# Gate and up with a fourth mixed pair per unit, and the first weight sum of a pair made by accumulating transfers

## The chip, the cores and the metric

The kernel runs on one core of one Trainium2 chip. The metric is the device time in microseconds (us) of one execution. Engines are named as in the profile: PE is the matmul engine (TensorE), DVE is VectorE, ACT is ScalarE, POOL is GpSimd, SP is SyncE, which here only issues loads.

## What is computed

A decoder trunk of two layers on 256 tokens of width 2048, float32. Layer 0 is a Mamba-2 mixer, layer 1 sliding-window attention, and each layer ends in the same feed-forward block, which is what the change touches:

```python
D_MODEL, SEQ, DEPTH, D_FF = 2048, 256, 2, 5632

def swiglu(u, w_gate, w_up, w_down):
    return (jax.nn.silu(u @ w_gate) * (u @ w_up)) @ w_down

for layer in range(DEPTH):
    ...                                                    # mixer or attention, norms, residual
    ffn = swiglu(rmsnorm(h, g[2]), ffn_w_gate[layer], ffn_w_up[layer], ffn_w_down[layer])
    h = h + rmsnorm(ffn, g[3])
```

## The kernel before

**Products.** Float32 accuracy is made of three matmuls: each weight tile and each activation tile is split into a high and a low part (hi = cast, lo = tile - hi), and a block product is hi x hi, hi x lo, lo x hi, each a 128x128 by 128x512 matmul. The high part of a weight is a cast on ACT into `whi` (L136), the low part a subtraction on DVE into `wlo` (L137). There are four buffers of each (`CVB`), and `Weights.next` converts up to three parts ahead of the one that PE uses. Raw weights come from memory through SP's queue into five buffers `raw` (`RAWB`), loaded up to four tiles ahead.

**Units.** Gate and up are done in 11 units of 512 columns per layer. The first unit is plain. In units 1 to 10 the 16 slices of the contraction (2048 = 16 x 128) form eight pairs 0 to 7 of an even and an odd slice. A plain pair is two items, "A" (gate) and "B" (up): each 2 slices x 2 halves of the tokens x 3 = 12 matmuls, from one raw tile of 512 KB and one conversion of 128x1024. A mixed pair, item "M", does the same 2x2x2 block product with seven products in the place of eight (Strassen's scheme): 21 matmuls. Its weights come in four parts that are converted one after the other:

- "a": gate's even slice and up's odd slice (raw tile `ta`), 6 matmuls
- "g": gate's odd slice (half of raw tile `tb`, whose other half is up's even slice), 3 matmuls
- "13": the tile `t13` = `ta` + up's even slice, added to both halves, 6 matmuls
- "24": the tile `t24`, first half `t13`'s first half + up's odd slice, second half that + gate's odd slice, 6 matmuls

The sums are three additions on DVE (L114, in `_sums`), issued right after the conversion of "g". `t13` and `t24` have one buffer each, in the pool `mixed` of the layer. The activations' mixed forms of each pair (`sx`) are computed once per layer by `mixed_x` and reused by all units; those calls are spread over the items of the first unit's "up" by a hook, every other item.

**Order.** The list `UNIT` sets the order on PE and thereby that of loads and conversions: A and B of pair 3, M0, A and B of 4, M1, A and B of 5, M2, then "E" (L447 to L451, where ACT and DVE combine finished products), then A and B of 6 and 7. After E, `store_half` transposes half of the last unit's result after each "B". A unit ends with four additions (L871), two SiLU (L873) and two products (L875).

**Queues.** SP issues all weight loads in order. POOL has only small work in these stages, and its queue's transfers are the spill and fetch of the residual `h` (L688, L695) outside of the units. Engines and queues run their instructions in order; a new use of a buffer waits until the last reader of the old contents has ended. The down projection and the mixer's output projection use mixed pairs too, with the same class `Weights`, and aren't touched.

Of the kernel before, what the change touches and what calls it, by code (L numbers as in the profile page):

```python
# [8 lines left out]
F32 = mybir.dt.float32  # L9
F32R = mybir.dt.float32r  # L10
AF = mybir.ActivationFunctionType
ALU = mybir.AluOpType
AX = mybir.AxisListType

P = 128
# [6 lines left out]
FF = 5632  # L22
KF = FF // P
EPS = 1e-6
NH = 64
CW = 512
# [1 line left out]
SUB = 2  # L28
RAWB = 5
CVB = 4  # L30
SPAIRS = 3


def both(*pairs):
    return [(c, i) for i in pairs for c in "AB"]
# [15 lines left out]

UNIT = both(3) + [("M", 0)] + both(4) + [("M", 1)] + both(5) + [("M", 2), ("E", 0)] + both(6, 7)
DOWN = [pair_order(KF, 6, 8, 3, 4), pair_order(KF, 8, 2, 2, 4)]
WOUT = [pair_order(DI // P, 3, 13, 3, 2), pair_order(DI // P, 6, 2, 2, 3)]

# [1 line left out]
class Weights:  # L59
# [6 lines left out]
    def __init__(self, nc, pool, specs, scaled, raw_ahead=RAWB - 1, cv_ahead=CVB - 1):  # L66
        self.nc, self.pool, self.specs, self.scaled = nc, pool, specs, scaled
        self.raw_ahead, self.cv_ahead = raw_ahead, cv_ahead
        self.subs, self.first = [], {}
        for i, (key, ap) in enumerate(specs):  # L70
            if isinstance(ap, tuple):
                if ap[0] == "b":
                    for part in ("a", "g", "13", "24"):
                        self.subs.append((i, part, SUB, CW, key + part))
                continue
            a = ap.shape[1]
            n = ap.shape[2]
            per = (SUB * CW) // n
            for s in range(0, a, per):
                self.first.setdefault(key, len(self.subs))  # L80
                self.subs.append((i, s, per, n, key))
        self.raw = []
        self.cv = []
        self.pin = lambda ins: ins
        self.pos = 0

    def _load(self, upto):
        while len(self.raw) < min(upto, len(self.specs)):
            key, ap = self.specs[len(self.raw)]
            if isinstance(ap, tuple):  # L90
                t = self.pool.tile([P, 2, CW], F32, tag="raw", name="raw", bufs=RAWB)
                for k in range(2):
                    self.nc.sync.dma_start(t[:, k : k + 1, :], ap[1 + k])
            else:
                _, a, n = ap.shape
                t = self.pool.tile([P, a, n], F32, tag="raw", name="raw", bufs=RAWB)
                self.nc.sync.dma_start(t[:], ap)
            self.raw.append(t)

    def _mixed(self, i, part):  # L100
# [2 lines left out]
        return {"a": lambda: ta[:], "g": lambda: tb[:, 0:1, :], "13": lambda: self.t13[:],  # L103
                "24": lambda: self.t24[:]}[part]()

    def _sums(self, i):

        ta, tb = self.raw[i - 1], self.raw[i]
        t13, t24 = [self.spool.tile([P, 2, CW], F32, tag="t%d" % n, name="t%d" % n) for n in (13, 24)]
        self.t13, self.t24 = t13, t24  # L110
        for o, p, q in ((t13[:], ta[:], tb[:, 1:2, :].broadcast_to([P, 2, CW])),
                        (t24[:, 0, :], t13[:, 0, :], ta[:, 1, :]),
                        (t24[:, 1, :], t24[:, 0, :], tb[:, 0, :])):
            self.keep(self.nc.vector.tensor_tensor(o, p, q, ALU.add))  # L114

    def _convert(self, upto):
# [42 lines left out]
def tile_yoco(ctx: ExitStack, tc: tile.TileContext, a: dict):  # L159
# [48 lines left out]
    def add_ffn(l):  # L208
        wg, wu = a["ffn_w_gate"][l], a["ffn_w_up"][l]
        for u in range(FF // CW):  # L210
            if u == 0:
                add("gate%d_%d" % (l, u), wg, KD, CW * u)
                add("up%d_%d" % (l, u), wu, KD, CW * u)
                continue
            add_pairs("unit%d_%d" % (l, u), UNIT, (wg, CW * u), (wu, CW * u))
        wd = a["ffn_w_down"][l]
# [16 lines left out]

    W = Weights(nc, wpool, specs, scaled)
    W.keep = tc.keep_in_program_order

    def bank():
        return psum.tile([P, CW], F32, tag="bank", name="bank")
# [142 lines left out]
    def mixed_x(x, i, o, tmp):  # L381


        y = tmp[:, 0, :].rearrange("p (k t) -> p k t", k=2)
        f = tmp[:, 1, :].rearrange("p (n t) -> p n t", n=4)
        ks = slice(SUB * i, SUB * i + 2)
        nc.vector.tensor_tensor(y, x[0][:, ks, :].bitcast(F32), x[1][:, ks, :].bitcast(F32), ALU.add)
        e0, e1, o0, o1 = y[:, 0, :P], y[:, 0, P:], y[:, 1, :P], y[:, 1, P:]
        for n, p, q in ((1, e1, o1), (3, e0, e1), (2, e0, f[:, 1, :]), (0, o0, f[:, 2, :])):
            nc.vector.tensor_tensor(f[:, n, :], p, q, ALU.subtract)  # L390
        split_bank(o[:, :, 0, :], o[:, :, 1, :], f)
# [165 lines left out]
    xt = new_xt()  # L557
# [253 lines left out]
    def row_factor():  # L811

        return [norm_stats(hpool, h[1], t) for t in range(NT)]
# [17 lines left out]
    def ffn(layer, mix):  # L831
        xt = new_xt()
        xh, xl, _ = xt
        with tc.tile_pool(name="ffn%d" % layer, bufs=1, side="right") as fp:
            hid = [fp.tile([P, KF, T], F32R, tag=n, name=n) for n in ("hh", "hl")]
            spool = tc.tile_pool(name="mixed%d" % layer, bufs=1, side="right")
            scr = hpool.tile([P, 2 * NT, CW], F32, tag="gpost", name="scr")
            todo = []

            def hook():  # L840
                if todo:
                    f = todo.pop(0)
                    if f is not None:
                        f()

            def store_half(u, t):

                pt = bank()
                for k in range(4):
                    nc.tensor.transpose(pt[:, P * k : P * (k + 1)], scr[:, NT + t, P * k : P * (k + 1)], ident[:])  # L850
                ts = slice(P * t, P * (t + 1))
                ks = slice(4 * u, 4 * u + 4)
                split_bank(hid[0][:, ks, ts], hid[1][:, ks, ts], pt[:].rearrange("p (k t) -> p k t", k=4))

            def store(u):
                for t in range(NT):
                    store_half(u, t)

            def unit(u):

                pp = Pairs("unit%d_%d" % (layer, u), UNIT, xt, lambda i: sx[:, i])
                terms = [scr[:, 0, :], scr[:, 1, :], vh[:, 0, :], vh[:, 1, :]]
                stores = []
                for n, item in enumerate(UNIT):
                    pp.item(item, terms)
                    if item[0] == "E":
                        stores = [0, 1]
                    elif stores and item[0] == "B":
                        store_half(u - 1, stores.pop(0))
                for name, part in zip(Pairs.OUT, terms):  # L870
                    nc.vector.tensor_tensor(part, pp.bk[name][:], part, ALU.add)  # L871
                for t in range(NT):
                    nc.scalar.activation(scr[:, t, :], scr[:, t, :], AF.Silu, scale=rs[t][:, 0:1])  # L873
                for t in range(NT):
                    nc.vector.scalar_tensor_tensor(scr[:, NT + t, :], vh[:, t, :], rs[t][:, 0:1], scr[:, t, :],  # L875
                                                   ALU.mult, ALU.mult)

            rs = None
            for u in range(FF // CW):
                if u:  # L880
                    unit(u)
                    continue
                gb = a_first("gate%d_%d" % (layer, u), mix, gt[:, layer, 2, :], xt)
                rs = row_factor()
                spill_h()
                sp = spool.__enter__()
                W.spool = sp
                sx = sp.tile([P, SPAIRS, 4, 2, P], F32R, tag="sx", name="sx")
                vh = sp.tile([P, 2, CW], F32, tag="vh", name="vh")
                for i in range(SPAIRS):  # L890
                    todo += [None, lambda i=i: mixed_x(xt, i, sx[:, i], sp.tile([P, 2, CW], F32, tag="t13", name="yf"))]
                for t in range(NT):
                    nc.scalar.activation(scr[:, t, :], gb[t][:], AF.Silu, scale=rs[t][:, 0:1])
                ub = a_form("up%d_%d" % (layer, u), xt, KD, hook=hook)
                for t in range(NT):
                    nc.vector.scalar_tensor_tensor(scr[:, NT + t, :], ub[t][:], rs[t][:, 0:1], scr[:, t, :],
                                                   ALU.mult, ALU.mult)
            spool.__exit__(None, None, None)
            spool = tc.tile_pool(name="down%d" % layer, bufs=1, side="right")
            W.spool = dp = spool.__enter__()  # L900
            todo += [None, lambda: store(FF // CW - 1)]

            def close():
                spool.__exit__(None, None, None)
                fetch_h()

            mix = Stage("down%d" % layer, DOWN, hid).run(Mix(layer, 3), dp, close, todo, 2 if layer == 0 else CVB)
            return mix
# [14 lines left out]
    with tc.tile_pool(name="attn", bufs=1, side="right") as ap:  # L923
        xt = new_xt()
# [506 lines left out]
```

## Time and profile before

| | |
|---|---|
| median of 3 runs | 2361.01 us (2360.69 to 2361.43) |
| the profiled execution's own time | 2360.69 us |
| its span, first to last instruction | 2358.8 us |
| PE busy | 2338.6 us, 99% |
| DVE busy | 2031.0 us, 86% |
| ACT busy | 1403.3 us, 59% |
| POOL busy | 91.3 us, 4% |
| DMA | 462.24 MB, mean 196 GB/s |

A row of a group of instructions reads: line, engine, operation, output <- inputs, shape, count, then busy us and mean ns of one, then the engine's idle time before them and what ended it. A row of the timeline reads: start in us, duration, engine, line, operation; in brackets the idle time before it and what ended that. A row of waits reads: who waited <- for whom: us in total, times, longest. A row of windows reads: stretch, its length, then busy us (and count) of PE, PEld (weight load into PE), DVE, ACT, POOL, then the granted clock of PE, the busy share of the DMA engines and GB/s. A row of one line's instructions gives minimum, median and maximum ns, then first and last start; "DMA to landing" is the time from issue until the data has landed.

### The profile page before, as it was taken

To read this page: it belongs to the slowest core of one execution; us is meant where nothing else is said; L and a number is where in the kernel's file an instruction comes from. 1 tells how busy PE (TensorE), PEld (TensorE's weight loads), DVE (VectorE), ACT (ScalarE), POOL (GpSimd) and SP (SyncE) were. 2 spreads that over 40 slices of the span, in tenths; PEclk is the share of its full clock that TensorE was granted. 3 is DMA by queue.
4 is the path that set the end of the run, shared out by engine and by line. 5 is a ranking of instruction groups with operands and counts; after the bars stand their busy time and mean duration, and the time that the engine had idled before them with its cause. 6 is when DMAs were issued, how large, how long until landed. Compare 5 with 4: busy or idle time off the path is not lost.

```text
span 2358.8 us, 32303 instructions
## 1 busy us (share of the span) xinstructions
PE 2338.6 (99%) x11519; PEld 1941.8 (82%) x11519; DVE 2031.0 (86%) x2878; ACT 1403.3 (59%) x1983; POOL 91.3 (4%) x76
## 2 busy tenths in 40 slices
PE   9999999999999999999999999999999999999998
PEld 8888888888878888888888878777888888888886
DVE  6998887878987999999998878965899999999786
ACT  6576766665565555555555567754555555555554
POOL 2500000000000000000000000000000000000000
PEclk9999999999999999999999999999999999999999
DMA  7576666657666666566666765436665665666675
GB/s 227 161 225 196 189 188 194 189 171 243 195 205 196 196 196 206 188 204 207 214 190 199 206 236 169 135 127 186 198 199 193 206 211 185 200 205 202 199 209 192
DMA packets 288673, 462.24 MB, mean 196 GB/s; under 512 B 20208, under 2 KB 118768, under 8 KB 286720
## 3 DMA queue, kind: packets, MB, share of 16 engines
q1 hardware_dynamic: 286752, 449.30, 61.3%
q0 software_dynamic: 1472, 10.55, 1.2%
q8 instruction: 90, 1.47, 0.3%
q14 instruction: 71, 0.58, 0.1%
q10 hardware_dynamic: 288, 0.33, 0.0%
HBM read 453.76 MB, written 6.36 MB: 195 GB/s over the span
## 4 chain that ended last, share of the span: by engine, by line
PE 94%; DVE 3%; ACT 1%; issue 1%; DMA 0%; POOL 0%; DVEq 0%; SPq 0%; ACTq 0%; POOLq 0%
PE bank L420 20%; PE bank L418 20%; PE bank L419 20%; PE bank L318 13%; PE bank L323 7%; PE bank L376 3%; PE bank L377 3%; PE bank L378 3%; DVE wlo L137 1%; PE bank L850 1%; PE bank L1119 1%; PE bank L1294 1%; DVE acc L1050 1%; PE bank L613 1%; PE bank L1330 0%
## 5 line engine op out<-in xcount | busy, mean ns | idle before, releaser
L137 DVE TENSOR_TENSOR wlo<-raw,whi 128x1024 fp32r<-128x1024 f32 (+1 forms) x785 | 883.6, 1155 | 162.9 <-ACT whi L136 154.7
L136 ACT CAST whi<-raw 128x1024 fp32r<-128x1024 f32 (+1 forms) x785 | 771.0, 999 | 422.1 <-PE bank L420 243.7
L318 PE MATMUL bank<-xx,whi 128*128 128x512 f32 (+1 forms) x1488 | 521.3, 396 | 0.0
L136 ACT CAST whi<-t 128x1024 fp32r<-128x1024 f32 x194 | 204.5, 1054 | 358.4 <-DVE t L114 230.0
L323 PE MATMUL bank<-xx,wlo 128*128 128x256 f32 (+1 forms) x1488 | 414.6, 284 | 0.9 <-DVE wlo L137 0.9
L418 PE MATMUL bank<-whi,xx 128*128 128x512 f32 x980 | 384.9, 393 | 0.0
L420 PE MATMUL bank<-whi,xx 128*128 128x512 f32 x980 | 382.1, 390 | 0.0
L419 PE MATMUL bank<-wlo,xx 128*128 128x512 f32 x980 | 381.6, 389 | 0.0
L318 PEld LDWEIGHTS bank<-xx,whi 128*128 128x128 f32 (+1 forms) x1488 | 275.7, 187 | 61.6 <-issue 0.3
L137 DVE TENSOR_TENSOR wlo<-t,whi 128x1024 fp32r<-128x1024 f32 x194 | 237.0, 1222 | 72.0 <-ACT whi L136 70.9
L323 PEld LDWEIGHTS bank<-xx,wlo 128*128 128x128 f32 (+1 forms) x1488 | 279.4, 188 | 11.5 <-issue 5.2
L418 PE MATMUL bank<-whi,hh 128*128 128x512 f32 x564 | 219.8, 390 | 0.0
L420 PE MATMUL bank<-whi,hl 128*128 128x512 f32 x564 | 219.4, 389 | 0.0
L419 PE MATMUL bank<-wlo,hh 128*128 128x512 f32 x564 | 219.4, 389 | 0.0
L420 PEld LDWEIGHTS bank<-whi,xx 128*128 128x128 f32 x980 | 184.0, 188 | 38.8
L419 PEld LDWEIGHTS bank<-wlo,xx 128*128 128x128 f32 x980 | 184.1, 188 | 37.4
L418 PEld LDWEIGHTS bank<-whi,xx 128*128 128x128 f32 x980 | 184.0, 188 | 37.0
L114 DVE TENSOR_TENSOR t<-t,raw 128x512 f32<-128x512 f32 x194 | 134.1, 691 | 5.8
L420 PEld LDWEIGHTS bank<-whi,hl 128*128 128x128 f32 x564 | 105.9, 188 | 22.2
L419 PEld LDWEIGHTS bank<-wlo,hh 128*128 128x128 f32 x564 | 105.9, 188 | 21.9
L418 PEld LDWEIGHTS bank<-whi,hh 128*128 128x128 f32 x564 | 105.9, 188 | 21.6
L114 DVE TENSOR_TENSOR t<-raw 128x1024 f32<-128x1024 f32 x97 | 118.2, 1218 | 0.0
(240 smaller groups left out, 3212.0 us busy)
## 6 DMA issues: line engine op xcount, KB each, us to landing
raw<-in_ssm_w_in_dram SPq DMA_DIRECT2D x161, 512.0 KB, 4.6
raw<-in_ffn_w_down_dram SPq DMA_DIRECT2D x120, 512.0 KB, 5.5
raw<-in_ffn_w_gate_dram SPq DMA_DIRECT2D x116, 512.0 KB, 4.7
raw<-in_ffn_w_up_dram SPq DMA_DIRECT2D x116, 512.0 KB, 3.9
raw<-in_ffn_w_gate_dram SPq DMA_DIRECT2D x120, 256.0 KB, 3.8
raw<-in_ffn_w_up_dram SPq DMA_DIRECT2D x120, 256.0 KB, 4.1
raw<-in_ffn_w_down_dram SPq DMA_DIRECT2D x112, 256.0 KB, 4.6
raw<-in_ssm_w_out_dram SPq DMA_DIRECT2D x46, 512.0 KB, 4.9
```

Of the source, the lines that this page charges most:

```text
L114: self.keep(self.nc.vector.tensor_tensor(o, p, q, ALU.add))
L136: self.pin(nc.scalar.copy(hi[:], src))
L137: self.pin(nc.vector.tensor_tensor(lo[:], src, hi[:].bitcast(F32), ALU.subtract))
L318: nc.tensor.matmul(o, wh, xx[:, kt, :, :].rearrange("p a t -> p (a t)"), start=(kt == 0), stop=(kt == kts - 1))
L323: nc.tensor.matmul(o[:, :T], wl, xx[:, kt, 0, :], start=False, stop=False)
L376: nc.tensor.matmul(o, sh, wh, start=(kt == 0), stop=False)
L377: nc.tensor.matmul(o, sh, wl, start=False, stop=False)
L378: nc.tensor.matmul(o, sl, wh, start=False, stop=(kt == kts - 1))
L418: nc.tensor.matmul(o, s[0], wh, start=(n == 1), stop=False)
L419: nc.tensor.matmul(o, s[0], wl, start=False, stop=False)
L420: nc.tensor.matmul(o, s[1], wh, start=False, stop=(n == self.total[name]))
L613: nc.tensor.matmul(o[:], hi[:, kk, cs], xr[2][:, kt, :, :].rearrange("p a t -> p (a t)"), start=(kt == 0), stop=(kt == KD - 1))
```

## The change

Pair 3 becomes a fourth mixed pair (the list before has pairs 0 to 2 mixed and 3 to 7 plain). The order of a unit becomes A4 B4 M0 A5 B5 M1 A6 M2 B6 M3 E A7 B7: pairs 0 to 3 are mixed, 4 to 7 plain. After E the halves of the last result are stored after A7 and after B7. `t13` is no longer added on DVE in units 1 to 10: when a pair's second raw tile is loaded, `_first_sums` has GpSimd's queue load gate's even and up's odd slice into `t13` (two transfers of 256 KB) and then add up's even slice to both halves with one accumulating transfer (512 KB). The two sums that give `t24` stay on DVE. The fourth pair's `sx` lies in the last four slices of the first hidden tile, which are written only by the last unit; `mixed_x` takes its scratch from `t24`'s buffer instead of `t13`'s and is called four times per layer instead of three. Down and output projections keep the addition on DVE.

```diff
-SPAIRS = 3
+SPAIRS = 4
...
-UNIT = both(3) + [("M", 0)] + both(4) + [("M", 1)] + both(5) + [("M", 2), ("E", 0)] + both(6, 7)
+UNIT = both(4) + [("M", 0)] + both(5) + [("M", 1), ("A", 6), ("M", 2), ("B", 6), ("M", 3), ("E", 0)] + both(7)
...
+        self.by_dma = set()
+        self.t13s = []
...
                     self.nc.sync.dma_start(t[:, k : k + 1, :], ap[1 + k])
+                if ap[0] == "b" and key in self.by_dma:
+                    self._first_sums(len(self.raw))
...
+    def _first_sums(self, i):
+
+        (_, ge, uo), (_, _, ue) = self.specs[i - 1][1], self.specs[i][1]
+        t13 = self.spool.tile([P, 2, CW], F32, tag="t13", name="t13")
+        for k, ap in enumerate((ge, uo)):
+            self.nc.gpsimd.dma_start(t13[:, k : k + 1, :], ap)
+        self.nc.gpsimd.dma_start(t13[:], ue.broadcast_to([P, 2, CW]), accum_op=ALU.add)
+        self.t13s.append(t13)
+
     def _sums(self, i):
 
         ta, tb = self.raw[i - 1], self.raw[i]
-        t13, t24 = [self.spool.tile([P, 2, CW], F32, tag="t%d" % n, name="t%d" % n) for n in (13, 24)]
+        if self.specs[i][0] in self.by_dma:
+            t13 = self.t13s.pop(0)
+        else:
+            t13 = self.spool.tile([P, 2, CW], F32, tag="t13", name="t13")
+            self.keep(self.nc.vector.tensor_tensor(t13[:], ta[:], tb[:, 1:2, :].broadcast_to([P, 2, CW]), ALU.add))
+        t24 = self.spool.tile([P, 2, CW], F32, tag="t24", name="t24")
         self.t13, self.t24 = t13, t24
-        for o, p, q in ((t13[:], ta[:], tb[:, 1:2, :].broadcast_to([P, 2, CW])),
-                        (t24[:, 0, :], t13[:, 0, :], ta[:, 1, :]),
-                        (t24[:, 1, :], t24[:, 0, :], tb[:, 0, :])):
+        for o, p, q in ((t24[:, 0, :], t13[:, 0, :], ta[:, 1, :]), (t24[:, 1, :], t24[:, 0, :], tb[:, 0, :])):
             self.keep(self.nc.vector.tensor_tensor(o, p, q, ALU.add))
...
+    W.by_dma = {"unit%d_%dM" % (l, u) for l in range(2) for u in range(1, FF // CW)}
...
-                pp = Pairs("unit%d_%d" % (layer, u), UNIT, xt, lambda i: sx[:, i])
+                pp = Pairs("unit%d_%d" % (layer, u), UNIT, xt, lambda i: sxs[i])
...
-                    elif stores and item[0] == "B":
+                    elif stores:
                         store_half(u - 1, stores.pop(0))
...
-                sx = sp.tile([P, SPAIRS, 4, 2, P], F32R, tag="sx", name="sx")
+                sx = sp.tile([P, SPAIRS - 1, 4, 2, P], F32R, tag="sx", name="sx")
+                sxs = [sx[:, i] for i in range(SPAIRS - 1)]
+                sxs.append(hid[0][:, KF - 4 : KF, :].rearrange("p k t -> p (k t)")
+                           .rearrange("p (a n t) -> p n a t", a=2, n=4))
...
-                    todo += [None, lambda i=i: mixed_x(xt, i, sx[:, i], sp.tile([P, 2, CW], F32, tag="t13", name="yf"))]
+                    todo += [None, lambda i=i: mixed_x(xt, i, sxs[i], sp.tile([P, 2, CW], F32, tag="t24", name="yf"))]
```

## The prediction

> **What bounds the kernel now.** I read the busy totals first, then who keeps the matmul engine waiting, then one unit of gate and up in order of time, then the DMA rows.
>
> ```profile
> span 2358.8 us, 32303 instructions
> PE 2338.6 (99%) x11519; PEld 1941.8 (82%) x11519; DVE 2031.0 (86%) x2878; ACT 1403.3 (59%) x1983; POOL 91.3 (4%) x76
> PE bank L376 <- ACT xx L297: 2.1, 5, 0.9
> PE bank L377 <- DVE wlo L137: 1.3, 1, 1.3
> ...
> 760.00:1160.00 400.00, 400.00 (x1801) 330.97 (x1801) 367.53 (x406) 227.05 (x255) 0.00 (x0) 1.00 0.62 200
> L447 ACT COPY scr<-bank x10: 576/576/577, 764.2 to 1146.3; 128x512 f32<-128x512 f32 x10
> ```
>
> PE is busy for 99%, and its two longest waits in total are 2.1 and 1.3 us. In the 400 us of the third view (units of layer 0; columns PE, PEld, DVE, ACT, POOL, granted clock, DMA share, GB/s) PE never rests, and VectorE (DVE) is busy for 367.53, 92%. The last row marks one step (E) of each of ten units: (1146.3 - 764.2)/9 = 42.45 us per unit. So a unit is bound by PE, with DVE close behind and GpSimd (POOL) empty. Now inside a unit:
>
> ```profile
> 997.32 0.39 PE L418 MATMUL bank<-whi,xx 128*128 128x512 f32 x1
> 999.36 0.39 PE L418 MATMUL bank<-whi,sx 128*128 128x512 f32 x1
> 1002.08 0.39 PE L418 MATMUL bank<-whi,xx 128*128 128x512 f32 x1
> 1004.80 0.39 PE L418 MATMUL bank<-whi,xx 128*128 128x512 f32 x1
> 1007.52 0.39 PE L418 MATMUL bank<-whi,xx 128*128 128x512 f32 x1
> ...
> 1005.28 1.42 DVE L114 TENSOR_TENSOR t<-t,raw 128x512 f32<-128x512 f32 x2
> 1006.61 1.22 DVE L137 TENSOR_TENSOR wlo<-t,whi 128x1024 fp32r<-128x1024 f32 x1
> ...
> 1005.35 1.05 ACT L136 CAST whi<-t 128x1024 fp32r<-128x1024 f32 x1 [2.45 <-DVE t L114]
> 1007.76 1.05 ACT L136 CAST whi<-t 128x1024 fp32r<-128x1024 f32 x1 [1.35 <-PE bank L420]
> ```
>
> M0 begins on PE at 997.32, its "13" part at 999.36 (9 matmuls later), A4 at 1002.08, B4 at 1004.80, M1 at 1007.52. A4 is 12 matmuls in 2.72 us, so one costs 0.2267 us (the 0.39 of a row is pipelined), a plain item 2.72 and a mixed pair of 21 matmuls 4.76. The last row tells how far ahead the conversions run: the cast of M1's "24" starts 0.24 us after B4 ends at 1007.52, since there are four whi buffers and it takes the one of four parts before.
>
> **The change, part by part.**
>
> *Matmuls.* Pair 3 as A and B is 24 matmuls, as a mixed pair 21. Three per unit, 20 units: 60 x 0.2267 = 13.6 us off PE, 0.68 per unit (42.45 to 41.77). That is the whole possible gain.
>
> *VectorE and ScalarE.* Durations:
>
> ```profile
> L137 DVE TENSOR_TENSOR wlo<-raw,whi 128x1024 fp32r<-128x1024 f32 (+1 forms) x785 | 883.6, 1155 | 162.9 <-ACT whi L136 154.7
> L114 DVE TENSOR_TENSOR t<-t,raw 128x512 f32<-128x512 f32 x194 | 134.1, 691 | 5.8
> L114 DVE TENSOR_TENSOR t<-raw 128x1024 f32<-128x1024 f32 x97 | 118.2, 1218 | 0.0
> ...
> 994.22 0.69 DVE L137 TENSOR_TENSOR wlo<-raw,whi 128x512 fp32r<-128x512 f32 x1
> ```
>
> Three old pairs lose the first sum: -3 x 1.218 = -3.65. The new pair brings 3 large and one half conversion instead of two: 1.155 + 0.69 = 1.85, and two sums 1.38: together +3.23. DVE per unit is 0.4 us lighter. ACT gets one cast of 1.05 us and one of half its size onto some 24 of 42 us (227.05 of 400): free.
>
> ```profile
> L387 DVE TENSOR_TENSOR yf<-hh,hl 128x512 f32<-128x512 f32 x16 | 11.0, 688 | 0.2
> L390 DVE TENSOR_TENSOR yf<-yf 128x128 f32<-128x128 f32 x112 | 29.0, 286 | 0.9
> L265 DVE TENSOR_TENSOR fx<-yf,fx 128x512 fp32r<-128x512 f32 x22 | 15.1, 684 | 0.0
> ...
> 703.00:740.00 37.00, 37.00 (x162) 30.58 (x161) 26.70 (x42) 16.51 (x20) 1.12 (x2) 0.98 0.67 212
> ```
>
> One more call of mixed_x per layer costs DVE 0.688 + 4 x 0.286 + 0.684 = 2.5 us and falls into the first "up", where DVE is busy for 26.70 of 37 us (703 to 740), beside PE; without that cover it would cost 5 us in all. That the two transposing steps now follow A7 and B7 costs nothing: the same eight transposes per unit.
>
> *The chain through POOL.* The tile t13 has one buffer. Its transfers for the next pair can only be issued when the last reader of this pair's t13 (wlo of "13", L137) has ended. Then POOL issues two loads of 256 KB, waits for both to land, issues the accumulating 512 KB, and only when that has landed can DVE make the two sums and wlo of "13", which PE needs. Behind POOL's waiting instruction stand the next pair's loads, and much later h's fetch (L695), which this doesn't reach; behind DVE's waiting sums stand wlo of "13" and "24" and the next items' wlo, and PE waits for those. On SP, loads queue for raw buffers that the late sums hold, five in all; one reload (4.6 us, below) fits into a period of the chain. No accumulating transfer is in the trace, so the nearest rows are the plain ones of these sizes in the same units and POOL's own:
>
> ```profile
> L688 POOL DMA_DIRECT2D hd<-h x4: 533/557/592, 689.5 to 1657.7; - x4
> DMA to landing us min/median/max: 4.2/4.3/4.6
> ...
> L93 SPq DMA_DIRECT2D raw<-in_ffn_w_gate_dram x57: 327/328/341, 740.8 to 1133.4; - x57
> DMA to landing us min/median/max: 2.6/4.0/5.1
> ...
> L97 SPq DMA_DIRECT2D raw<-in_ffn_w_up_dram x48: 367/378/379, 746.5 to 1143.6; - x48
> DMA to landing us min/median/max: 3.6/4.6/7.0
> ```
>
> 256 KB (L93) land in 2.6 to 5.1 us, 512 KB (L97) in 3.6 to 7.0; POOL's own 1024 KB stores in 4.2 to 4.6, and POOL takes 0.56 to issue one. SP's medians hold a queue of SP's own transfers, POOL's queue is empty; so I take halfway between minimum and median: 3.3 and 4.1. Chain C = 0.56 + 3.3 + 4.1 = 8.0 us. Ends: the minima, 0.56 + 2.6 + 3.6 = 6.8; the medians, 9.2; and if accumulating doubles the landing of its 512 KB (it has to read t13 too), 0.56 + 3.3 + 8.2 = 12.1. Taking it as plain is a choice by the nearest row. From landing, DVE needs 1.33 (two sums, 1005.28 to 1006.61) and 1.22 (wlo), with two signals some 2.7; so the "13" parts of two pairs can't follow closer than C + 2.7 = 10.7 us.
>
> The Trainium skill (DMA: Bandwidth & Descriptors, Anatomy of one DMA — SWDGE (gpsimd) path) fits such a transfer as 2.0 us plus bytes over 436 GB/s. The trace's minimum for 256 KB agrees with it (2.6 both), that for 512 KB does not (3.6 against an estimated 3.2). By it C is an estimated 6.4, and the sum below would come to 2412.
>
> *What PE allows.* With one plain item between pairs (M1, A6, M2, B6, M3) PE goes from "13" to "13" in 6 + 6 + 12 + 6 + 3 = 33 matmuls, 7.48 us; from M0 to M1 (A5 and B5 between) in 45, 10.2. Each is below 10.7. Lead helps once per unit only: four buffers let wlo of "13" end at most 2.2 us ahead of PE, and at M0 hardly that, as the end of a unit shows:
>
> ```profile
> 1019.04 1.23 DVE L137 TENSOR_TENSOR wlo<-t,whi 128x1024 fp32r<-128x1024 f32 x1 [1.02 <-ACT whi L136]
> 1020.48 3.49 DVE L137 TENSOR_TENSOR wlo<-raw,whi 128x1024 fp32r<-128x1024 f32 x3 [0.21 <-ACT whi L136]
> ...
> 1029.20 1.23 DVE L137 TENSOR_TENSOR wlo<-raw,whi 128x1024 fp32r<-128x1024 f32 x1 [0.44 <-ACT whi L136]
> 1032.41 1.23 DVE L137 TENSOR_TENSOR wlo<-raw,whi 128x1024 fp32r<-128x1024 f32 x1 [0.19 <-ACT whi L136]
> ...
> 1039.96 2.40 DVE L137 TENSOR_TENSOR wlo<-t,whi 128x1024 fp32r<-128x1024 f32 x2
> ```
>
> From wlo of M2's "24" (ends 1020.27) to wlo of the next M0's "13" (about 1041.18) DVE is idle for only 0.21 + 0.44 + 0.19 = 0.84 of 20.9 us. After the change that stretch loses two wlo (2 x 1.16, from the 3.49 of three) and one first sum (1.22): 20.07 - 2.32 - 1.22 = 16.5; with the wlo of M3's own "24", 1.23, it is 17.7 us from wlo of M3's "13" to wlo of the next M0's "13". PE needs 12 + 48 + 9 matmuls there and eight transposes (0.96, what 183 matmuls leave of 42.45), 16.6 us: DVE ends last.
>
> *The sum.* Unit = 3 x 10.7 + 17.7 = 49.8 us against 42.45: +7.35, times 20 = +147. The PE gain is inside it. Against the profiled execution's own 2360.69 (span 2358.8 and 1.9 around it; 0.3 under the median of three, 2361.01) that gives 2508.
>
> *The clock.* After a wait this trace shows:
>
> ```profile
> 700.52 0.50 PE L377 MATMUL bank<-wlo,xx 128*128 128x512 f32 x1 [1.28 <-DVE wlo L137]
> 701.59 0.63 PE L377 MATMUL bank<-wlo,xx 128*128 128x512 f32 x1
> 702.02 0.63 PE L378 MATMUL bank<-whi,xx 128*128 128x512 f32 x1
> ...
> 1394.00:1396.00 2.00, 0.90 (x3) 0.47 (x4) 1.95 (x5) 1.67 (x6) 1.41 (x5) 1.00 0.06 15
> ```
>
> Matmuls 0.43 us apart instead of 0.2267 after 700.52; in the two us from 1394, of which PE rests for 1.10, the clock stays 1.00. The waits foreseen, about 3 us before M2 and M3, may do the first. A half-speed stretch of eight matmuls adds 1.6 us; between pairs the chain hides it, after M3 it would cost up to 1.6 x 20 = 32 us. I take 0, by the second row, and keep 32 for the range.
>
> **Rivals.**
>
> *Faster: the chain is hidden.* If C is short enough, the 0.68 per unit is gained: 2347. It decides at 3 x (C + 2.7) + 17.7 = 42.45, C = 5.55. For it: POOL is empty, DVE gets lighter. Against: the minima give 6.8. It needs transfers faster than any row of their size, or pairs converted farther ahead than four buffers allow. Chance 0.12.
>
> *Landings at their fastest rows.* C = 6.8: unit 3 x 9.5 + 17.7 = 46.2, +75, 2436. For it: nothing is ahead in POOL's queue, and while PE waits, SP's loads rest as well. The skill's fit, above, points here and a little past it. Chance 0.20, including the still shorter chains down to 2400.
>
> *Accumulating costs double.* C = 12.1: 3 x 14.8 + 17.7 = 62.1, +393, 2754. No row speaks for it but the second read. Chance 0.08, beyond 2600.
>
> *DMA engines full.* Per unit 8.4 MB become 12.6, or 14.7 with the second read.
>
> ```profile
> 1386.00:1390.00 4.00, 4.00 (x20) 3.30 (x19) 2.15 (x4) 1.34 (x2) 0.00 (x0) 1.00 1.04 402
> ```
>
> At 402 GB/s that is 31 to 37 us, within a unit; at the units' own 200/0.62 = 323 GB/s, 14.7 MB take 45.5, +61 in all, 2422. In a unit of 49.8 it fits at either rate; it would lengthen the landings rather than bound by itself. I count it in the ranges.
>
> **How the numbers follow.** Chain-bound with C from 7 to 9.5: 0.60, predicted 2508, with its own range 2450 to 2600. The fastest rows 0.20, double 0.08, hidden 0.12. 2400 to 2600 leaves out 0.20. A change of 0.2%, some 5 us, is about what can be told from none. Faster 0.11 (hidden), same 0.02 (a chain near 5.5), slower 0.87.
>
> **What would show it.** PE's rows: 60 matmuls fewer, 11,459. Waits: PE idle for wlo of "13" twice or more per unit, DVE's sums (t24) released by a DMA into t13, together over 100 us. POOL: 4 x 3 x 20 = 240 transfer issues, each accumulating one waiting for the loads. E to E about 50 us. The first sums 20 x 3 = 60 fewer (37 left); DVE's stretch from M3 to M0 near 17.7. If E to E is 41.8, I am wrong in C; if PE waits for something other than wlo of "13" and "24", in the mechanism; if the granted clock falls below 0.95 in the units, in the term that I took as 0.

## The result, and the profile after

The changed kernel takes 2811.85 us (median of 4; 2807.19 to 2816.56) against 2360.85: a ratio of 1.191, 95% interval 1.190 to 1.193. That is 451 us slower; 2508 was forecast, with 2600 as the upper end. The page, waits of PE, ACT and DVE, and one step (E) of each of ten units:

```profile
span 2810.8 us, 33020 instructions
PE 2509.1 (89%) x11459; PEld 2008.7 (71%) x11459; DVE 2019.7 (72%) x2910; ACT 1426.9 (51%) x2025; POOL 280.1 (10%) x316
...
PE 48%; DMA 31%; DVE 11%; issue 6%; ACT 3%; POOL 2%; DVEq 0%; POOLq 0%; ACTq 0%; SPq 0%
DMA t<-in_ffn_w_up_dram 30%; PE bank L335 10%; PE bank L436 8%; PE bank L437 8%; PE bank L435 7%; DVE wlo L153 5%; PE bank L340 5%; PE bank L393 2%; PE bank L394 2%; PE bank L395 2%; DVE t L130 2%; POOL t L115 2%; ACT whi L152 1%; DVE acc L1071 1%; PE bank L1315 0%
...
PE bank L435 <- ACT whi L152: 235.2, 124, 5.2
PE bank L436 <- DVE wlo L153: 46.6, 54, 2.2
...
ACT whi L152 <- DMA t<-in_ffn_w_up_dram: 474.5, 74, 9.8
DVE t L130 <- DMA t<-in_ffn_w_up_dram: 444.8, 60, 8.6
...
L464 ACT COPY scr<-bank x10: 587/587/587, 780.1 to 1367.5; 128x512 f32<-128x512 f32 x10
```

PE has its 60 matmuls fewer (11,459), and is idle for 11% of the span. The third line is the chain that ended last, by engine, the fourth by line: transfers into a tile `t` from "up" now have 30% of it. Before, PE had 94%:

```profile
PE 94%; DVE 3%; ACT 1%; issue 1%; DMA 0%; POOL 0%; DVEq 0%; SPq 0%; ACTq 0%; POOLq 0%
```

L435 to L437 are the old L418 to L420, L152 and L153 the casts and wlo, L130 the two sums, L464 is E. PE's longest waits are for casts of ACT (235.2 us), fewer for wlo (46.6); ACT's casts and DVE's sums both wait for the accumulating transfer. A unit takes (1367.5 - 780.1)/9 = 65.27 us instead of 42.45; 20 x 22.8 = 456 us, so the units account for all of the 451 lost. Inside one unit, POOL's timeline and the rows of DVE and PE that answer it:

```profile
1003.45 0.58 POOL L115 DMA_DIRECT2D t<-in_ffn_w_gate_dram  x1 [14.73 <-DVE wlo L153]
1004.02 0.57 POOL L115 DMA_DIRECT2D t<-in_ffn_w_up_dram  x1
1009.55 1.22 POOL L116 DMA_DIRECT2D t<-in_ffn_w_up_dram  x1 [4.96 <-DMA t<-in_ffn_w_up_dram]
1019.88 0.58 POOL L115 DMA_DIRECT2D t<-in_ffn_w_gate_dram  x1 [9.11 <-DVE wlo L153]
...
1024.87 1.22 POOL L116 DMA_DIRECT2D t<-in_ffn_w_up_dram  x1 [3.85 <-DMA t<-in_ffn_w_up_dram]
1033.70 0.58 POOL L115 DMA_DIRECT2D t<-in_ffn_w_gate_dram  x1 [7.61 <-DVE wlo L153]
...
1039.17 1.22 POOL L116 DMA_DIRECT2D t<-in_ffn_w_up_dram  x1 [3.78 <-DMA t<-in_ffn_w_up_dram]
1047.94 0.58 POOL L115 DMA_DIRECT2D t<-in_ffn_w_gate_dram  x1 [7.54 <-DVE wlo L153]
...
1068.25 0.58 POOL L115 DMA_DIRECT2D t<-in_ffn_w_gate_dram  x1 [14.24 <-DVE wlo L153]
...
1017.03 1.42 DVE L130 TENSOR_TENSOR t<-t,raw 128x512 f32<-128x512 f32 x2 [7.11 <-DMA t<-in_ffn_w_up_dram]
...
1030.85 1.42 DVE L130 TENSOR_TENSOR t<-t,raw 128x512 f32<-128x512 f32 x2 [7.12 <-DMA t<-in_ffn_w_up_dram]
...
1045.09 1.42 DVE L130 TENSOR_TENSOR t<-t,raw 128x512 f32<-128x512 f32 x2 [7.53 <-DMA t<-in_ffn_w_up_dram]
...
1018.14 0.80 PE L435 MATMUL bank<-whi,sx 128*128 128x512 f32 x1 [2.92 <-ACT whi L152]
...
1023.22 0.63 PE L435 MATMUL bank<-whi,xx 128*128 128x512 f32 x1
1023.64 0.63 PE L436 MATMUL bank<-wlo,xx 128*128 128x512 f32 x1
```

Read in order of time it is the forecast chain. POOL waits for wlo of "13" (the bracket at L115), issues two loads, waits for them (the bracket at L116), issues the accumulating transfer; DVE sits idle until that lands, and PE behind it. For M1, M2 and M3: loads to accumulating issue 6.10, 4.99, 5.47 us; issue to landing 7.48, 5.98, 5.92; landing to the next loads 2.85 each time. The periods are 16.4, 13.8 and 14.2 us, and 20.3 from the end of M3's "13" to that of the next M0. The last two rows are the half-speed clock, 0.43 us apart, after PE's wait.

The accumulating transfer, L116, by itself, and the 6 us from 1039, in which it runs almost alone (the busy share of the DMA engines in tenths, then GB/s, in 40 slices of 0.15 us):

```profile
L116 POOL DMA_DIRECT2D t<-in_ffn_w_up_dram x80: 1207/1227/1260, 712.5 to 2551.0; - x80
DMA to landing us min/median/max: 5.8/6.6/10.2
...
DMA  6442221100000099876998989999999999951000
GB/s 232 178 191 109 109 109 41 55 14 0 0 0 0 0 150 68 109 96 109 109 137 123 150 137 177 177 218 218 205 205 191 205 218 191 178 96 27 0 0 0
...
q0 software_dynamic: 272, 0.52, 56.8%
```

It lands in 5.8 us at best. In the eleven slices from the 25th on the engines are 90% busy or more and move 177 to 218 GB/s, about half of the 402 quoted in the prediction.

### The profile page after: what moved, and what is told of

It reads as the page before. It is cut to its first block, busy times and chain, and to the rows that moved or that the text cites. A ratio compares the mean times of both kernels' runs of the same rounds, so it can differ in the third digit from the quotient of the medians.

```text
span 2810.8 us, 33020 instructions
## 1 busy us (share of the span) xinstructions
PE 2509.1 (89%) x11459; PEld 2008.7 (71%) x11459; DVE 2019.7 (72%) x2910; ACT 1426.9 (51%) x2025; POOL 280.1 (10%) x316
## 4 chain that ended last, share of the span: by engine, by line
PE 48%; DMA 31%; DVE 11%; issue 6%; ACT 3%; POOL 2%; DVEq 0%; POOLq 0%; ACTq 0%; SPq 0%
DMA t<-in_ffn_w_up_dram 30%; PE bank L335 10%; PE bank L436 8%; PE bank L437 8%; PE bank L435 7%; DVE wlo L153 5%; PE bank L340 5%; PE bank L393 2%; PE bank L394 2%; PE bank L395 2%; DVE t L130 2%; POOL t L115 2%; ACT whi L152 1%; DVE acc L1071 1%; PE bank L1315 0%
## 5 line engine op out<-in xcount | busy, mean ns | idle before, releaser
L153 DVE TENSOR_TENSOR wlo<-raw,whi 128x1024 fp32r<-128x1024 f32 (+1 forms) x785 | 870.6, 1140 | 156.8 <-ACT whi L152 152.8
L152 ACT CAST whi<-raw 128x1024 fp32r<-128x1024 f32 (+1 forms) x785 | 756.1, 985 | 395.5 <-PE bank L437 230.9
L152 ACT CAST whi<-t 128x1024 fp32r<-128x1024 f32 x234 | 245.4, 1049 | 715.7 <-DMA t<-in_ffn_w_up_dram 474.5
L130 DVE TENSOR_TENSOR t<-t,raw 128x512 f32<-128x512 f32 x234 | 161.4, 690 | 448.6 <-DMA t<-in_ffn_w_up_dram 444.8
L436 PE MATMUL bank<-wlo,xx 128*128 128x512 f32 x880 | 354.8, 403 | 16.6 <-DVE wlo L153 16.6
L435 PE MATMUL bank<-whi,xx 128*128 128x512 f32 x880 | 360.1, 418 | 2.4 <-ACT whi L152 2.4
L437 PE MATMUL bank<-whi,xx 128*128 128x512 f32 x880 | 350.7, 398 | 0.0
L435 PE MATMUL bank<-whi,hh 128*128 128x512 f32 x644 | 260.2, 410 | 80.7 <-ACT whi L152 80.7
L153 DVE TENSOR_TENSOR wlo<-t,whi 128x1024 fp32r<-128x1024 f32 x234 | 285.6, 1220 | 54.2 <-ACT whi L152 52.1
L436 PE MATMUL bank<-wlo,hh 128*128 128x512 f32 x644 | 263.9, 410 | 0.1
L435 PE MATMUL bank<-whi,sx 128*128 128x512 f32 x240 | 122.3, 524 | 152.1 <-ACT whi L152 152.1
L437 PE MATMUL bank<-whi,hl 128*128 128x512 f32 x564 | 219.5, 389 | 0.0
L435 PEld LDWEIGHTS bank<-whi,xx 128*128 128x128 f32 x880 | 180.4, 205 | 50.7 <-ACT whi L152 10.3
L435 PEld LDWEIGHTS bank<-whi,hh 128*128 128x128 f32 x644 | 122.3, 193 | 119.5 <-ACT whi L152 96.5
L437 PEld LDWEIGHTS bank<-whi,xx 128*128 128x128 f32 x880 | 171.5, 195 | 37.6
L435 PEld LDWEIGHTS bank<-whi,sx 128*128 128x128 f32 x240 | 54.3, 233 | 196.3 <-ACT whi L152 188.1
L436 PE MATMUL bank<-wlo,sx 128*128 128x512 f32 x240 | 127.8, 533 | 30.1 <-DVE wlo L153 30.0
```

The source lines that it names most:

```text
L152: self.pin(nc.scalar.copy(hi[:], src))
L153: self.pin(nc.vector.tensor_tensor(lo[:], src, hi[:].bitcast(F32), ALU.subtract))
L435: nc.tensor.matmul(o, s[0], wh, start=(n == 1), stop=False)
L436: nc.tensor.matmul(o, s[0], wl, start=False, stop=False)
L437: nc.tensor.matmul(o, s[1], wh, start=False, stop=(n == self.total[name]))
```

## The experiments

Two theories stood against the chain: that the added bytes fill the DMA engines (bandwidth), and that four pairs close together with E late overload DVE (order). Each run is given with its median, its ratio to the kernel before on the same chip, and the unit time read from E as above.

### Two buffers for t13

```diff
+        t13 = self.spool.tile([P, 2, CW], F32, tag="t13", name="t13", bufs=2)
...
-                sx = sp.tile([P, SPAIRS - 1, 4, 2, P], F32R, tag="sx", name="sx")
+                sx = sp.tile([P, SPAIRS - 2, 4, 2, P], F32R, tag="sx", name="sx")
```

> The changed kernel with two buffers for t13 (the room comes from the third pair's mixed activations, which move into the last four slices of the second hidden tile). Same transfers, same bytes, same order; only the wait of POOL's loads for the last reader of the one t13 is taken away. Theory chain (one buffer makes load, load, accumulate, two sums, conversion a serial chain of 14 to 16 us per pair): the chain runs two pairs ahead and is hidden; time falls to between 2347 (all of the 60 matmuls won) and 2430. Theory bandwidth (the added bytes fill the DMA engines): the DMA share of 0.70 over a unit of 65.3 us is 45.7 us of engine time per unit, so a unit cannot be shorter than that: 2361 + 20 x (45.7 - 42.45) = 2426 or more. Theory order (four pairs close together, E late, DVE behind): time stays above 2700.

2466.33 us, 1.045 (1.043 to 1.046), unit 48.32. One more buffer takes 345 of the 451 us away with the same transfers. So bandwidth alone is refuted as the main cause. But the time is 36 us above the range of the chain theory, where bandwidth allowed 2426 or more. The windows of the changed kernel, of this one and of the next (columns as in the section on the profile before):

```profile
800.00:1160.00 360.00, 282.78 (x1034) 211.68 (x1032) 207.99 (x239) 137.47 (x159) 51.99 (x66) 0.87 0.69 191
```
```profile
800.00:1160.00 360.00, 331.54 (x1401) 255.94 (x1400) 283.82 (x325) 188.15 (x218) 70.76 (x90) 0.99 0.90 263
...
DMA to landing us min/median/max: 3.4/7.4/11.1
```
```profile
800.00:1160.00 360.00, 349.68 (x1545) 282.00 (x1544) 352.99 (x394) 206.44 (x239) 0.00 (x0) 1.00 0.60 192
```

With two buffers the DMA share is 0.90 and POOL's 256 KB loads land in 7.4 us (median) instead of 3.9. POOL still waits for each pair's loads before it issues their sum and then the next loads, 543.6 us in this trace; busy engines and POOL's waiting in order are not told apart by this run.

### The fourth pair and the new order alone, all sums on DVE

```diff
-    W.by_dma = {"unit%d_%dM" % (l, u) for l in range(2) for u in range(1, FF // CW)}
```

> The changed kernel with the first sums back on DVE in all units (no transfers on POOL's queue there): the fourth pair and the new order alone. Theory chain: no chain; DVE has 39.1 + 3.2 + 1.2 = 43.5 us of work per unit against 41.8 on PE, so DVE bounds the unit at 43 to 44.5: 2370 to 2400. Theory order: most of the 451 us remain, above 2700.

2387.38 us, 1.011 (1.010 to 1.013), unit 43.89, as forecast: the third window has DVE busy for 352.99 of 360 us. The fourth pair and the order together cost 27 us with all the sums on DVE, not 451; the order by itself was not run.

### The transfers alone, in the order of before

```diff
-SPAIRS = 4
+SPAIRS = 3
...
+UNIT = both(3) + [("M", 0)] + both(4) + [("M", 1)] + both(5) + [("M", 2), ("E", 0)] + both(6, 7)
```

> Three mixed pairs in the order of before, with the first sums by accumulating transfers on POOL's queue (one buffer): the transfers alone. Theory chain: two items lie between pairs, so PE allows 10.2 us from pair to pair where the chain needs 13.8 to 16: a unit of 42.45 + 2 x 4 to 6 plus 2 at its end, 52 to 56: 2550 to 2640. Theory order: at or below 2361. Theory bandwidth: share x time per unit of 0.61 x 42.45 plus 0.75 x (45.7 - 26) = 41 us, still under PE: about 2361.

2558.23 us, 1.082 (1.078 to 1.086), unit 52.46. The chain costs some 200 us where three pairs stand two items apart, as the chain theory foresaw.

### A plain third transfer, one buffer and two

```diff
-        self.nc.gpsimd.dma_start(t13[:], ue.broadcast_to([P, 2, CW]), accum_op=ALU.add)
+        self.nc.gpsimd.dma_start(t13[:], ue.broadcast_to([P, 2, CW]))
```

> The changed kernel with the third transfer as a plain one (it overwrites t13 instead of adding to it, so the sums are left out). Same number of transfers, waits and bytes written. If the accumulation itself is slow (the transfer lands in 5.8 to 6.6 us where a plain 512 KB load lands in 3.6 to 4.6), landing falls by some 2 us and with it four periods per unit: 2812 - 20 x 4 x 2 = 2650. If the wait for the loads and the issue are what costs, landing stays near 6 us and the time near 2800.

2668.79 us (one run, no interval), unit 58.26. The same row for it:

```profile
L116 POOL DMA_DIRECT2D t<-in_ffn_w_up_dram x80: 712/712/726, 710.1 to 2410.3; - x80
DMA to landing us min/median/max: 4.0/4.9/7.3
```

Adding costs 1.7 us of landing (6.6 against 4.9), of which 0.5 is POOL's own issue (1.23 against 0.71), 6.8 us over the four pairs of a unit; the unit is 7.0 us shorter. That is a third of the loss; the other two thirds are there with plain transfers.

> Two buffers for t13 and the third transfer plain (the addition and so the right sums are left out). Bandwidth as what is left with two buffers: in the changed kernel a unit takes 0.70 x 65.27 = 45.7 us of the DMA engines, with a plain third transfer 0.66 x 58.26 = 38.4; if the 105 us that the two-buffer kernel stays behind are the DMA engines (share 0.90 there), a unit comes back to 42 to 44 us: 2350 to 2395, at a share near 0.9. If the 105 us are latency of the chain or the order of DVE's work, landing is 1.7 us shorter per pair but the time stays above 2430.

2404.34 us, 1.019 (1.017 to 1.020), unit 44.77, share 0.84. Of the 105 us that two buffers leave, 62 go with the cheaper transfer, though as many transfers and waits remain. It lightens the DMA engines (0.84 against 0.90) and ends below the 2430 named for latency, which speaks for the engines; but POOL's wait for the loads is shorter too (463.8 us against 543.6), so latency isn't ruled out. It ends 9 us above the range named, and what that is was not separated.

### No third transfer

```diff
-        self.nc.gpsimd.dma_start(t13[:], ue.broadcast_to([P, 2, CW]), accum_op=ALU.add)
```

> The changed kernel without the third transfer (up's even slice is not added to t13, so the sums lack it); the two loads and the single buffer stay. Theory chain: C is then the pair of loads alone, some 5.0 us, a period of 5.0 + 2.85 = 7.9 against PE's 7.5 and 10.2, so only 0.4 us of wait per period is left: a unit of about 43.5, 2370 to 2400 with the order's own cost. If the single buffer or the order and not the length of the chain were at fault, it stays above 2500.

2416.48 us, 1.024 (1.022 to 1.027), unit 45.70. With one stage in the chain instead of two, and still one buffer, 395 of the 451 us are gone. It misses the range by 16; its loads take 3.0 to 6.9 us to land, not a steady 5, which may be why.

### Matmuls that fill the waits

```diff
+                    if part == "g" and key[:4] == "unit" and i in (1, 2, 3):
+                        for _ in range(10):
+                            tc.keep_in_program_order(nc.tensor.matmul(bk["p2"][:], Pairs.zero[:], hi[:, 0, :],
+                                                                      start=False, stop=False))
```

Room for the zero tile is made as for the second buffer, by moving a pair's mixed activations.

> The changed kernel with ten extra matmuls by a zero tile ahead of the 13 part of M1, M2 and M3 in every unit (they add nothing to the result): 10 x 0.2267 = 2.3 us of PE work in each of three waits of 3 to 5 us, so PE rests for less. Theory clock (the half-speed stretches after the waits cost time of their own, about 2.4 us per unit between M3 and the next M0, where the chain does not hide them): the granted clock rises from 0.87 in the units towards 1.0 and the time falls by up to 20 x 2.4 = 48 us, to 2765 or so. Theory chain alone: the half-speed stretches lie beside the chain, so the time stays within 10 us of 2812 whatever the clock; if the fillers were on the path, it rises by up to 20 x 3 x 2.3 = 136.

2755.94 us, 1.167 (1.165 to 1.169), unit 62.24: with 600 matmuls more the kernel is 56 us faster, 8 more than the clock theory allowed. POOL's timeline in it, and the window:

```profile
894.64 0.58 POOL L115 DMA_DIRECT2D t<-in_ffn_w_gate_dram  x1 [7.55 <-DVE wlo L153]
...
908.56 0.58 POOL L115 DMA_DIRECT2D t<-in_ffn_w_gate_dram  x1 [7.66 <-DVE wlo L153]
...
925.46 0.58 POOL L115 DMA_DIRECT2D t<-in_ffn_w_gate_dram  x1 [10.63 <-DVE wlo L153]
...
941.92 0.58 POOL L115 DMA_DIRECT2D t<-in_ffn_w_gate_dram  x1 [9.34 <-DVE wlo L153]
...
760.00:1360.00 600.00, 525.33 (x2102) 410.57 (x2101) 370.45 (x427) 242.01 (x280) 88.74 (x112) 0.93 0.72 202
```

The periods between pairs stay (13.9 from 894.64 to 908.56, 16.5 from 925.46 to 941.92); the stretch from M3 to M0 falls from 20.3 to 16.9 us, and the granted clock in these 600 us is 0.93 against 0.87. So between pairs the chain hides the slow clock. After M3 two things differ, as rows of the changed kernel show:

```profile
1047.70 0.79 PE L435 MATMUL bank<-whi,hh 128*128 128x512 f32 x1 [0.30 <-ACT whi L152]
...
1062.24 1.06 ACT L152 CAST whi<-t 128x1024 fp32r<-128x1024 f32 x1 [3.08 <-DMA t<-in_ffn_w_up_dram]
1063.20 1.33 ACT L890 ACTIVATE scr<-scr,rs 128x512 f32<-128x512 f32 x2
1063.95 1.42 DVE L892 SCALAR_TENSOR_TENSOR scr<-vh,rs,scr 128x512 f32<-128x512 f32 x2 [1.08 <-ACT scr L890]
```

The first is the clock: from 1047.70 to 1051.92 PE does eight matmuls and three transposes in 4.2 us; at full speed they would take an estimated 2.2 (8 x 0.2267 + 3 x 0.12, the costs worked out in the prediction), so some 2 us are lost. The second is an order on ACT: the SiLU of the unit (L890) stands behind the cast of M0's "13", which waits for M0's transfer, and DVE waits for the SiLU, 1.08 us here and 28.6 in the whole trace. In the kernel with the fillers the SiLU stands ahead of that cast (it starts at 919.74, the cast at 922.85), and DVE doesn't wait for it. How the 56 us divide between the clock and this order was not separated.

### In search of a faster version

The five below keep four pairs and take the first sum off DVE in other ways. First GpSimd's own addition, for four pairs and for M0 and M2 only:

```diff
+            self.keep(self.nc.gpsimd.tensor_tensor(t13[:], ta[:], tb[:, 1:2, :].broadcast_to([P, 2, CW]), ALU.add))
```

> Four pairs in the changed order, the first sum as an addition on GpSimd itself (no transfers). DVE: 43.9 us per unit with all sums on it, less 4 x 1.22 = 39.0, under PE's 41.8. GpSimd's row for 128x512 is 1.3 to 2.0 us, so 128x1024 takes some 2.6 to 4, a chain of about 4 + 2.7 us per pair against PE's 7.5. Theory chain: short enough, PE bounds: 2347 to 2365. Theory order (four pairs close together and E late cost by themselves): stays near 2387. If the two engines hinder each other on SBUF, DVE's durations grow and it lands between.

2487.99 us, 1.054 (1.052 to 1.055), unit 49.26, above every time named.

> As the addition on GpSimd, but for M0 and M2 only; M1 and M3 on DVE. DVE 41.5 us per unit, about PE's 41.8, so 2350 to 2375; if GpSimd's additions slow DVE down, this loses half of that and comes out ahead of the one with four.

2430.52 us, 1.030 (1.028 to 1.031), unit 46.44, about half of the loss with four additions. Both are worse than all sums on DVE. Groups of DVE and POOL with all sums on DVE, then with four on GpSimd, in the same 360 us:

```profile
L153 DVE TENSOR_TENSOR wlo<-raw,whi 128x1024 fp32r<-128x1024 f32 (+1 forms) x132 | 137.1, 1085 | 1.2
L153 DVE TENSOR_TENSOR wlo<-t,whi 128x1024 fp32r<-128x1024 f32 x67 | 81.8, 1222 | 3.6 <-ACT whi L152 2.1
```
```profile
L152 DVE TENSOR_TENSOR wlo<-raw,whi 128x1024 fp32r<-128x1024 f32 (+1 forms) x116 | 150.6, 1342 | 1.7 <-ACT whi L151 1.5
L152 DVE TENSOR_TENSOR wlo<-t,whi 128x1024 fp32r<-128x1024 f32 x60 | 91.9, 1532 | 34.0 <-ACT whi L151 34.0
L122 POOL TENSOR_TENSOR t<-raw 128x1024 f32<-128x1024 f32 x30 | 80.7, 2691 | 282.4 <-DMA raw<-in_ffn_w_up_dram 229.9 <-DVE wlo L152 52.5
```

DVE's conversions grow by 116 x 0.257 + 60 x 0.310 = 48 us over 30 additions of GpSimd: each takes 1.6 us from DVE, more than the 1.22 that the sum had cost there. The Trainium skill (SBUF — State Buffer, Who interferes with whom) says that a VectorE instruction with two SBUF inputs contends with a GpSimd instruction that reads SBUF; these rows agree, and the size is theirs.

Then accumulating transfers for M0 and M2 only, into a buffer of their own, 17.7 us and more apart (room for it is made as for the second buffer):

```diff
-                if ap[0] == "b" and key in self.by_dma:
+                if ap[0] == "b" and key in self.by_dma and ap[3] in (0, 2):
```

> Four pairs, accumulating transfers for M0 and M2 only, into a buffer of their own; M1 and M3 summed on DVE. Theory chain: from M0 to M2 PE takes 10.2 + 7.5 = 17.7 us and from M2 to the next M0 24, both above C + 2.7 = 14 to 16, so no wait; DVE 43.9 - 2 x 1.22 = 41.5 per unit, DMA engines some 35 us: 2347 to 2375. Theory bandwidth: half of the 105 us that two buffers leave, about 2410.

2384.69 us, 1.010 (1.009 to 1.012), unit 43.86: ACT's waits for a transfer into `t13` are down to 3.2 us in 360, but it ends 10 us over the range. In M0 and M2 wlo of "13" now ran between the two sums, so that the cast of "24" and its wlo came 1.2 us late:

```profile
916.74 0.68 DVE L130 TENSOR_TENSOR t<-t,raw 128x512 f32<-128x512 f32 x1
917.34 1.22 DVE L153 TENSOR_TENSOR wlo<-t,whi 128x1024 fp32r<-128x1024 f32 x1
918.48 0.68 DVE L130 TENSOR_TENSOR t<-t,raw 128x512 f32<-128x512 f32 x1
920.35 1.23 DVE L153 TENSOR_TENSOR wlo<-t,whi 128x1024 fp32r<-128x1024 f32 x1 [1.19 <-ACT whi L152]
```

Holding it behind both, and in another run also moving E forward:

```diff
-                self.pin(nc.vector.tensor_tensor(lo[:], src, hi[:].bitcast(F32), ALU.subtract))
+                (self.keep if s == "13" else self.pin)(nc.vector.tensor_tensor(lo[:], src, hi[:].bitcast(F32), ALU.subtract))
```

> The half-and-half kernel (transfers for M0 and M2) with one thing changed: wlo of 13 held behind both sums, so that the cast and wlo of 24 do not wait for the second sum. That removes 1.2 us of DVE's idle time twice per unit: up to 2.4 x 20 = 48 us if DVE decides, so 2347 to 2370; if E and the end of the unit decide, it stays at 2385.

2374.14 us, 1.006 (1.005 to 1.007), unit 42.90.

```diff
+UNIT = both(4) + [("M", 0), ("A", 5), ("M", 1), ("B", 5), ("M", 2), ("A", 6), ("M", 3), ("E", 0), ("B", 6)] + both(7)
```

> Four mixed pairs, accumulating transfers for M0 and M2 only into a buffer of their own, wlo of 13 held behind both sums, and E with four items behind it as in the kernel before: A4 B4 M0 A5 M1 B5 M2 A6 M3 E B6 A7 B7. If the 24 us that the half-and-half kernel loses come from E and the unit's last work falling together on DVE, and from the 1.2 us that wlo of 24 waits in M0 and M2, this is PE-bound: 2347 to 2362. If DVE's 41.5 of 41.8 us per unit leave no room in any order, 2370 to 2390. M0 to M2 is only 15 us here, against C + 2.85 of about 15, so some waits for the transfer may return: then above 2390.

2380.79 us, 1.009 (1.008 to 1.011), unit 43.80. The first won 10 us of at most 48; the second gave 7 of them back. None of these versions beats the kernel before, whose unit is 42.45.

## Why the prediction was wrong

**Direction and mechanism: right, but for one wait.** The single t13 buffer makes wlo, loads, accumulation, sums and wlo one serial chain. The second buffer (-345 us), the missing third transfer (-395) and the sums back on DVE (-424) each show it, and the rows of one unit are the forecast chain. (In these three the SiLU also stands ahead of the cast of M0's "13"; DVE's 28.6 us of waits for it are small beside them.) The prediction had PE wait for wlo and named any other wait as a sign against its mechanism. PE waits longest for the cast of ACT, 235.2 us against 46.6. The cast waits for the same landing as the sums, and POOL's next loads wait for wlo as forecast, so the chain stands; the cast was left out of it.

**The step that failed: the size of C.** C was taken as 8.0 us: 0.56 + 3.3 for the loads and 4.1 for the accumulating transfer. The three chains above give 5.5 and 6.5 on average, 12.0 in all. The loads were priced near SP's fastest rows, on the ground that POOL's queue is empty. Yet they start when SP reloads raw tiles freed by the same wait (DMA share 0.86 to 0.97 in the 5 or 6 us around each), and they land in 3.9 (median; 3.1 at best), near SP's median (that this is the reason was not tried by itself); the second one issues 0.57 later. The accumulation was priced as a plain load; it issues in 1.23 us, lands in 6.6, and moves its bytes at about half the rate. That was named as a rival, at 12.1 us and 2754, with a chance of 0.08 "beyond 2600". The chance was the error: "no row speaks for it but the second read" was a reason for it, not against it. But that 12.1 is so near the measured 12.0 is luck: its 8.2 for the accumulation is 1.7 too long, its 3.9 for the loads 1.6 too short. With the measured chain the formula gives 3 x (12.0 + 2.85) + 17.7 = 62.2 against 65.3 measured.

**The clock: taken as 0, wrong.** The granted clock is 0.87 in the units, below the 0.95 named as the sign. The remaining 3.1 us per unit are the stretch from M3 to M0, 20.3 to 20.8 instead of 17.7. In the unit shown PE loses some 2 us there to the slow clock, an estimated 40 us over 20 units where 32 was kept as the upper bound, and DVE waits 1.1 us for a SiLU that the transfer holds up on ACT, which the prediction didn't see. The fillers bring the stretch to 16.9 and the time down by 56 us; in the unit shown of that kernel PE does the stretch at full clock and DVE has no such wait.

**DVE and PE: right.** 60 matmuls fewer; DVE lighter by nothing that matters (2019.7 against 2031.0). The fourth pair and the order together cost 27 us in the kernel with all sums on DVE, whose unit of 43.89 us is near the 43.5 us of DVE work that the expectation named. The 0.68 us per unit on PE were won nowhere.

**Bandwidth** was put into the ranges as no bound in itself. True for the changed kernel (share 0.69); with two buffers, at 0.90, it is the likely next bound.

Put in one sum, with 44.5 for the three measured periods: (44.5 - 32.1) + (20.8 - 17.7) = 15.5 us per unit, 310 in all, against 304 between forecast and measurement.

## What to carry to other kernels

A sum made by transfers is not off the path because the engine that issues them is idle: count the stages that wait for one another (here free, load, accumulate, use) and put the whole chain against the time between two uses of the buffer; one more buffer was worth 345 us, more than any change of the transfers themselves but leaving one out. An operation that no row shows should not be priced as the nearest plain one without a wide range: here it landed in 6.6 us against 4.9. In this kernel, with DVE 92% busy beside PE at 100%, three matmuls fewer per unit were won in none of the versions, since no way of lightening DVE came free.

## What the runs showed of the hardware

- An accumulating transfer of 512 KB on GpSimd's queue lands in 6.6 us against 4.9 for a plain one of the same shape, takes 1.23 us to issue against 0.71, and moves 177 to 218 GB/s while the engines are 90% busy or more.
- A GpSimd addition of 128x1024 (2.69 us) beside DVE's conversions costs DVE 1.6 us.
- PE's clock was at half after a wait of 2.9 us (at 1018.14) and still at full after one of 2.4 (at 1031.93). In the kernel with the fillers it was at half after two waits of 1.25 and 1.00 us with one matmul between (at 942). That kernel, with 600 matmuls that compute nothing, was 56 us faster; how much of it is the clock was not separated.
